# Spreading softmax merge factors: twelve transposes of repeated columns, or one transpose, a store to DRAM and broadcast loads

## The chip, the cores and the metric

The kernel runs on one core of a Trainium2 chip. The metric is device time in microseconds (us) of one execution. Engines are named as in the profile: PE (TensorE matmuls; PEld its weight loads), DVE (VectorE), ACT (ScalarE), POOL (GpSimd) and SP (SyncE, which here only issues DMAs). Each takes its own queue of instructions in order and waits on semaphores where an instruction needs the result of another engine. SBUF is the memory on the chip with 128 partitions, PSUM the eight banks into which PE writes, DRAM the memory outside.

## The reference

Two decoder layers over 1024 tokens of width 1024, in float32. Layer 0 is a gating mixer followed by a squared-ReLU MLP; layer 1 is an attention mixer followed by the same kind of MLP. The change lies in the attention mixer. It has 8 heads of width 64 and three groups of keys (window 128 with stride 1, 512 with stride 4, 2048 with stride 16). For every token and head, each group g gives an unnormalised sum of values, a denominator and a row maximum, and the groups are merged:

```
m_all = jnp.max(jnp.stack(maxs), axis=0)
scales = [jnp.exp(m_ - m_all) for m_ in maxs]
num_sum = sum(n_ * c[..., None] for n_, c in zip(nums, scales))
den_sum = sum(d_ * c for d_, c in zip(dens, scales))
o = (num_sum / den_sum[..., None])
```

So a token's 64 values of a head and group are all multiplied by one number, the factor f = scale / den_sum.

## The kernel before

Heads are taken in pairs hp = 0 to 3, so that a pair's 2 x 64 = 128 channels fill the partitions. A pair and a group is a unit (`U`, with `u.hp`, `u.g`); there are 12 units, and within a pair they come in the order g = 1, 2, 0. For each unit PE forms queries, keys and values from the weights `in_w_qkv` (tiles `mm`, weight halves `wp`, by a scheme of seven products per pair of tiles); these are 128x512 matmuls that keep PE filled. Beside them runs the attention of the units, in steps of 256 tokens: `scores` (PE, tiles `at<-k,q`), the row maxima and exponentials (DVE line 1265, ACT line 1267, tile `st`), `turned` (PE transposes of the probabilities, then a split into a high and a low part, tiles `tr`), and `values` (PE, `at<-tr,V`, then ACT and DVE into the unit's `N`, lines 1304 and 1305). `N` holds channels on partitions and tokens along the row. The factors come from DVE the other way: `f` holds tokens on partitions.

`merge(hp, i)` does the merge of a pair for the token half i (512 tokens, four blocks of 128). It first forms `f` (lines 1402 to 1416), three groups x four blocks x two heads = 24 numbers for each of 128 partitions. To turn them, `factors(g)` lets ACT write each number 64 times side by side (line 1422, 128x512), and `spread_factors` lets PE transpose four 128x128 blocks of that into a PSUM bank, which then holds for each channel (partition) and token the factor. DVE multiplies by it (lines 1439 and 1450), sums the three groups (1443, 1451), and SP stores the result to DRAM (1456) for pairs 0 to 2; pair 3 is split for the output projection. The 8 merges thus hold 8 x 3 x 4 = 96 transposes.

Two things set the order. PE's is written out by hand: a planner (`Flow`) keeps a clock of PE's work, and a generator such as `merge` says with `yield` how many nanoseconds (the table `LAT`) to let pass before its next PE instruction. The attention of the next pair takes its `N` buffer once `merged[hp, 1]` has come. The other engines' order is made by a scheduler when the program is built. Temporary tiles `t` rotate through 11 buffers, `at` through 5 PSUM banks, raw weights `r` through 4 buffers: SP's weight loads (line 169) wait in its queue until DVE has split an earlier one.

## Time and profile before

| | |
|---|---|
| median of 3 runs | 2153.97 us (2151.77 to 2154.95) |
| the profiled execution | 2152.68 us, span 2151.0 us |
| mean granted TensorE clock | 0.992 |
| attention stage | about 956 to 1500 us of the span |
| transposes of tiles `t` (line 187) | 472, from 956 to 1477 us |
| ACT's broadcast copies of `f` (line 1422) | 24, from 1062 to 1472 us |

Busy times are from one profiled execution. A row of a timeline or a group has start or count, length, engine, line, operation, output<-input and shape; what stands in square brackets is idle time of the engine just before, and who ended it. Matmuls overlap, so the recorded length of one is more than what it adds. A wait for several semaphores is put down to the one that came last. For a DMA the time to landing runs from its issue to its completion.

### The profile page before, as it was taken

Reading aid. Unit: us, or ns where it says so; the run is one execution under the profiler, and the core shown is the slowest. Engines: PE = TensorE matmul, PEld = TensorE weight load, DVE = VectorE, ACT = ScalarE, POOL = GpSimd, SP = SyncE. Lnnn points to the kernel's source line nnn. Section 1 sums busy time; section 2 is a strip of 40 time slices with the busy share of each in tenths; the row PEclk is TensorE's granted clock in tenths of the full one; section 3 lists DMA queues with packets and bytes.
Section 4 is the critical chain, followed back from the end, with each engine's and each line's share of the span. In section 5 each row is a group of like instructions: output and inputs, shape, how many; then the busy total and the mean of one; then the engine's idle time right before and its main releaser. Section 6 shows DMA issues by size and latency. Waiting matters only on the chain.

```text
span 2151.0 us, 30121 instructions
## 1 busy us (share of the span) xinstructions
PE 2114.8 (98%) x10242; PEld 1752.0 (81%) x10242; DVE 1636.2 (76%) x3010; ACT 1121.3 (52%) x2261; POOL 562.8 (26%) x417
## 2 busy tenths in 40 slices
PE   8999999999999999999999999999999999999998
PEld 7888887888878888887888788887888888788887
DVE  7975268567699888897787877877866766988886
ACT  7644136555564444346665666664455556544443
POOL 2100113233223333521212122201133332332345
PEclk9999999999999999999999999999999999999999
DMA  6411113455364444221112111150055543644432
GB/s 223 141 59 50 40 47 134 165 189 184 114 195 153 156 157 137 89 93 37 46 46 56 40 47 47 44 182 27 32 176 195 191 158 123 200 153 141 144 106 78
DMA packets 158813, 247.04 MB, mean 115 GB/s; under 512 B 33481, under 2 KB 47940, under 8 KB 158660
## 3 DMA queue, kind: packets, MB, share of 16 engines
q1 hardware_dynamic: 158336, 244.94, 35.1%
q8 instruction: 80, 1.31, 0.3%
q14 instruction: 73, 0.60, 0.1%
q10 hardware_dynamic: 324, 0.18, 0.0%
HBM read 180.41 MB, written 64.66 MB: 114 GB/s over the span
## 4 chain that ended last, share of the span: by engine, by line
PE 87%; DVE 7%; ACT 2%; DMA 2%; issue 2%; SPq 1%; DVEq 0%; ACTq 0%
PE at L180 43%; PE mm L180 41%; PE at L187 2%; DVE wp L206 1%; DMA t<-hid 1%; DVE hx L206 1%; ACT t L1267 1%; DMA r<-in_w_up 1%; DVE h L935 1%; DVE k L1170 0%; DVE q L1170 0%; ACT wp L205 0%; SPq L169 0%; DVE tr L206 0%; DVE h L338 0%
## 5 line engine op out<-in xcount | busy, mean ns | idle before, releaser
L205 ACT ACTIVATE wp<-r 128x512 fp32r<-128x512 f32 (+3 forms) x490 | 294.2, 605 | 450.8 <-PE at L180 289.1
L180 PE MATMUL at<-hx,wp 128*128 128x512 f32 x1770 | 413.8, 389 | 4.6 <-DVE wp L206 2.6
L206 DVE TENSOR_TENSOR wp<-r,wp 128x512 fp32r<-128x512 f32 (+3 forms) x490 | 376.2, 771 | 38.6 <-ACT wp L205 34.9
L180 PE MATMUL mm<-y,wp 128*128 128x512 f32 x1608 | 399.3, 394 | 2.2 <-ACT t L1127 1.0
L180 PEld LDWEIGHTS at<-hx,wp 128*128 128x128 f32 x1770 | 331.8, 188 | 75.8 <-DVE h L935 3.7
L180 PEld LDWEIGHTS mm<-y,wp 128*128 128x128 f32 x1608 | 300.1, 189 | 68.1 <-DVE h L338 1.6
L180 PE MATMUL at<-t,wp 128*128 128x512 f32 x1344 | 314.0, 389 | 0.0
L180 PEld LDWEIGHTS at<-t,wp 128*128 128x128 f32 x1344 | 252.2, 188 | 52.7 <-DVE t L798 0.4
L408 POOL TENSOR_TENSOR t<-r 128x512 f32<-128x512 f32 (+3 forms) x78 | 112.8, 1446 | 677.8 <-DMA r<-in_w_dn 299.2
L410 POOL TENSOR_TENSOR r<-r 128x512 f32<-128x512 f32 (+3 forms) x77 | 115.0, 1493 | 388.7 <-DVE wp L206 352.7
L180 PE MATMUL mm<-t,wp 128*128 128x512 f32 x768 | 192.9, 399 | 0.0
L206 DVE TENSOR_TENSOR hx<-t,hx 128x512 fp32r<-128x512 f32 x192 | 178.5, 942 | 5.9 <-ACT hx L205 5.9
L180 PE MATMUL mm<-hx,wp 128*128 128x512 f32 x708 | 171.7, 389 | 0.1
L180 PEld LDWEIGHTS mm<-t,wp 128*128 128x128 f32 x768 | 141.4, 189 | 30.1 <-issue 0.2
L267 POOL TENSOR_TENSOR t<-t 128x512 f32<-128x512 f32 (+1 forms) x54 | 71.5, 1325 | 354.6 <-ACT t L258 352.9
L180 PE MATMUL mm<-y,whi 128*128 128x512 f32 x512 | 158.3, 390 | 0.0
L180 PEld LDWEIGHTS mm<-hx,wp 128*128 128x128 f32 x708 | 132.7, 188 | 28.1 <-DVE b L961 0.7
L935 DVE TENSOR_TENSOR h<-h,at 128x512 f32<-128x512 f32 x144 | 97.6, 680 | 55.3 <-PE at L180 55.3
L798 DVE TENSOR_TENSOR t<-t,at 128x512 f32<-128x512 f32 x116 | 79.2, 684 | 77.5 <-PE at L180 77.3
L180 PE MATMUL at<-y,wp 128*128 128x512 f32 x552 | 138.1, 391 | 0.0
L205 ACT ACTIVATE hx<-t 128x512 fp32r<-128x512 f32 x192 | 118.3, 629 | 30.6 <-DMA t<-hid 24.1
L413 POOL TENSOR_TENSOR r<-r 128x512 f32<-128x512 f32 (+3 forms) x77 | 105.4, 1369 | 82.7 <-issue 48.2
(221 smaller groups left out, 3198.8 us busy)
## 6 DMA issues: line engine op xcount, KB each, us to landing
t<-hid SPq DMA_DIRECT2D x194, 256.0 KB, 5.1
hid<-t SPq DMA_DIRECT2D x140, 256.0 KB, 2.5
r<-in_w_up SPq DMA_DIRECT2D x128, 256.0 KB, 2.8
r<-in_w_dn SPq DMA_DIRECT2D x88, 256.0 KB, 2.7
r<-in_w_qkv SPq DMA_DIRECT2D x72, 256.0 KB, 2.6
hid<-b SPq DMA_DIRECT2D x56, 256.0 KB, 2.7
r<-in_w_v SPq DMA_DIRECT2D x48, 256.0 KB, 3.9
h<-in_xT SPq DMA_DIRECT2D x16, 256.0 KB, 3.3
```

Source lines behind the costliest of these rows:

```text
L180: nc.tensor.matmul(out, lhsT, rhs, **kw)
L187: nc.tensor.transpose(out, src, ident)
L205: nc.scalar.activation(hi, src, AF.Copy)
L206: nc.vector.tensor_tensor(lo, src, hi.bitcast(F32), op=ALU.subtract)
L267: nc.gpsimd.tensor_tensor(self.acc, self.acc, sq, op=ALU.add)
L408: tt(r7, r[0, 0], r[1, 0], op=ALU.subtract)
L410: tt(r6, r[1, 0], r[0, 0], op=ALU.subtract)
L413: tt(r3, r[0, 1], r6, op=ALU.subtract)
L798: nc.vector.tensor_tensor(out, x, y, op=ALU.add)
L935: engine.tensor_tensor(hs[i, s], hs[i, s], src, op=ALU.add)
L1267: nc.scalar.activation(p[:, c], p[:, c], AF.Exp, bias=m, scale=-1.0, accum_out=dn)
```

## The change

For pairs 0 to 2, `merge` keeps the 24 numbers as one row of 24 columns (`fs`), and PE transposes all of them at once: out come 24 rows of 128 tokens. ACT copies them to SBUF (`ft`), SP stores them to a small DRAM tile (`rows`, 6 rows of 512 tokens: a group and a head each), and SP loads each row back to 64 partitions, two loads for a tile `t` of 128 partitions. DVE multiplies with these tiles in SBUF in place of a PSUM bank. The waits of the planner between the steps are written anew, the last two operations of DVE no longer have a raised priority, and pair 3 stays as it was. Per merge 12 transposes and three 128x512 copies of ACT go; one transpose, one 24x128 copy, one store of 12 KB and six loads of 128 KB come.

```diff
--- before.py
+++ after.py
@@ -1401,10 +1401,11 @@
         mn = small.tile([P, 4, 2], F32, tag="mn", name="mn", bufs=2)
         nc.vector.tensor_tensor(mn, e[0][:, :, :, 0], e[1][:, :, :, 0], op=ALU.min)
         nc.vector.tensor_tensor(mn, mn, e[2][:, :, :, 0], op=ALU.min)
-        f = small.tile([P, 3, 4, 2], F32, tag="f", name="f", bufs=2)
+        fs = small.tile([P, 3, 8], F32, tag="f", name="f", bufs=2)
+        f = fs.rearrange("p g (a b) -> p g b a", a=2) if hp < 3 else fs.rearrange("p g (b a) -> p g b a", a=2)
         for g in range(3):
             nc.vector.tensor_tensor(f[:, g], mn, e[g][:, :, :, 0], op=ALU.subtract)
-        nc.scalar.activation(f, f, AF.Exp)
+        nc.scalar.activation(fs, fs, AF.Exp)
         dn = small.tile([P, 4, 2], F32, tag="dn", name="dn", bufs=2)
         d2 = small.tile([P, 4, 2], F32, tag="d2", name="d2", bufs=2)
         nc.vector.tensor_tensor(dn, f[:, 0], e[0][:, :, :, 1], op=ALU.mult)
@@ -1415,6 +1416,41 @@
         for g in range(3):
             nc.vector.tensor_tensor(f[:, g], f[:, g], dn, op=ALU.mult)
         quick.__exit__(None, None, None)
+        if hp < 3:
+            yield LAT["merge"] + 1500
+            pt = at_bank()
+            transpose(pt[0:24, 0:P], fs.rearrange("p g n -> p (g n)"))
+            ft = small.tile([24, P], F32, tag="ft", name="ft", bufs=1)
+            rows = dram.tile([6, HALF], F32, tag=f"rows{i}", name=f"rows{i}", bufs=1)
+            with tc.high_priority(offset=PRIO):
+                nc.scalar.activation(ft, pt[0:24, 0:P], AF.Copy)
+            nc.sync.dma_start(rows.rearrange("n (b t) -> (n b) t", b=4), ft)
+            yield 5000
+
+            def row(g):
+                x = temp()
+                for a in range(2):
+                    nc.sync.dma_start(x[64 * a:64 * a + 64, :], rows[2 * g + a:2 * g + a + 1, :].partition_broadcast(64))
+                return x
+
+            pbs = [row(1), row(2)]
+            yield 4000
+            for g, pb in zip((1, 2), pbs):
+                nc.vector.tensor_tensor(own(pb, g), permuted(us_[g].N, i, g), own(pb, g), op=ALU.mult)
+            rest = pbs[0]
+            nc.vector.tensor_tensor(rest, rest, pbs[1], op=ALU.add)
+            pb = row(0)
+            yield 3000
+            yield valued[hp, i], 500
+            N = us_[0].N[:, half(i)]
+            nc.vector.tensor_tensor(N, N, pb, op=ALU.mult)
+            nc.vector.tensor_tensor(N, N, rest, op=ALU.add)
+            yield LAT["sum"]
+            if i == 0:
+                kept_N[hp] = dram.tile([P, S], F32, tag=f"N{hp}", name=f"N{hp}", bufs=1)
+            nc.sync.dma_start(kept_N[hp][:, half(i)], N)
+            merged[hp, i].t = flow.t
+            return
         yield LAT["merge"]
         def factors(g):
             fe = temp()
@@ -1430,7 +1466,7 @@
             return pb
 
         rest = None
-        fe_ns = LAT["fe"] * (1.0 if hp == 3 else LAT["fex"])
+        fe_ns = LAT["fe"]
         for g in (1, 2):
             fe = factors(g)
             yield fe_ns
@@ -1450,12 +1486,7 @@
             nc.vector.tensor_tensor(N, N, pb, op=ALU.mult)
             nc.vector.tensor_tensor(N, N, rest, op=ALU.add)
         yield LAT["sum"]
-        if hp < 3:
-            if i == 0:
-                kept_N[hp] = dram.tile([P, S], F32, tag=f"N{hp}", name=f"N{hp}", bufs=1)
-            nc.sync.dma_start(kept_N[hp][:, half(i)], N)
-        else:
-            split_N(hp, i, N)
+        split_N(hp, i, N)
         merged[hp, i].t = flow.t
 
     outs = {}
```

The planner lays PE's work out anew around the merges. In the order of PE, at the first merge (pair 0, half 0; `t_8784` and the like are inputs of the query, key and value products, `tr` probabilities), before:

```order
L180 MATMUL mm<-t_8784,wp 128x512 x3
L180 MATMUL mm<-t_8787,wp 128x512 x3
L180 MATMUL mm<-t_8658,wp 128x512 x3
L187 MATMUL at<-ident,t 128x128 x4
L180 MATMUL mm<-t_8674,wp 128x512 x3
L180 MATMUL mm<-t_8690,wp 128x512 x3
L180 MATMUL mm<-t_8702,wp 128x512 x3
L187 MATMUL at<-ident,t 128x128 x4
L180 MATMUL at<-tr,V 128x256 x2
```

and with the change:

```order
L180 MATMUL mm<-t_8784,wp 128x512 x3
L180 MATMUL mm<-t_8787,wp 128x512 x3
L187 MATMUL at<-ident,f 24x128
L180 MATMUL mm<-t_8658,wp 128x512 x3
L187 MATMUL at<-ident,t 128x128 x4
L180 MATMUL mm<-t_8674,wp 128x512 x3
L180 MATMUL mm<-t_8690,wp 128x512 x3
L180 MATMUL mm<-t_8702,wp 128x512 x3
L180 MATMUL mm<-y,wp 128x512 x3
```

The one transpose of `f` stands 12 matmuls of 512 columns and a group of transposes (that of V) ahead of where the first group of factors stood, and that group is gone. In the order of DVE, a little later in the same merge, before:

```order
L1439 TENSOR_TENSOR t<-N,at 128x512
L1443 TENSOR_TENSOR t<-t 128x512
L1202 TENSOR_TENSOR t<-t,mm 128x512
L206 TENSOR_TENSOR wp<-r,wp 128x512
L206 TENSOR_TENSOR tr<-at,tr 128x512 x2
```

and with the change:

```order
L1202 TENSOR_TENSOR t<-t,mm 128x512
L206 TENSOR_TENSOR wp<-r,wp 128x512
L1439 TENSOR_TENSOR t<-N,t 128x512
L206 TENSOR_TENSOR wp<-r,wp 128x512
L1439 TENSOR_TENSOR t<-N,t 128x512
L1441 TENSOR_TENSOR t<-t 128x512
L206 TENSOR_TENSOR tr<-at,tr 128x512 x2
```

Both multiplies (line 1439) now stand between a reduction of scores and the split of the probabilities `tr`; before, the first of them stood ahead of the reduction. In the order of SP, for the two merges of pair 0, with the change (`bvec` is the bias table, `N_10047` the result):

```order
L169 DMA r<-in_w_qkv 128x512
L1427 DMA rows_9770<-ft 24x128
L1433 DMA t<-rows_9770 64x512 x4
L169 DMA r<-in_w_qkv 128x512 x2
L1433 DMA t<-rows_9770 64x512 x2
L169 DMA r<-in_w_qkv 128x512
L1451 DMA N_10047<-N 128x512
L169 DMA r<-in_w_qkv 128x512
L1427 DMA rows_10123<-ft 24x128
L1433 DMA t<-rows_10123 64x512
L1066 DMA t<-bvec 64x2x64 x2
L1433 DMA t<-rows_10123 64x512 x5
```

Before, only the weight loads, the bias loads and the stores of `N` stood there; the stores and loads of `rows` are new, and share the queue with the weight loads.

## The prediction

> **What bounds the kernel now.** First the page: engines and the chain of waits.
>
> ```profile
> span 2151.0 us, 30121 instructions
> PE 2114.8 (98%) x10242; PEld 1752.0 (81%) x10242; DVE 1636.2 (76%) x3010; ACT 1121.3 (52%) x2261; POOL 562.8 (26%) x417
> ...
> PE 87%; DVE 7%; ACT 2%; DMA 2%; issue 2%; SPq 1%; DVEq 0%; ACTq 0%
> ```
>
> PE is busy for 98% of the span and holds 87% of the chain that ended last. The change touches one stage, so next the table by stretches, for the attention stage (columns: stretch, length, busy time of PE, PEld, DVE, ACT, POOL, then PE clock, DMA share, GB/s), and what PE waited for there (total us, times, longest).
>
> ```profile
> 956.00:1500.00 544.00, 529.27 (x3079) 440.80 (x3078) 438.94 (x1097) 337.95 (x868) 93.81 (x65) 0.98 0.20 58
> ```
> ```profile
> PE at L180 <- DVE tr L206: 3.5, 4, 1.1
> PE at L180 <- DVE q L1170: 2.4, 3, 1.0
> PE at L187 <- ACT t L1422: 2.1, 1, 2.1
> ```
>
> In this stage PE idles 544 - 529.27 = 14.7 us, in pieces of at most 2.1 us, and DVE is busy 439 of 544 us (81%), ACT 62%, the DMA engines 20%. So PE bounds the stage, with DVE not far behind it, and an instruction taken off PE shortens the span unless another engine then makes PE wait. The profiled execution took 2152.68 us, 1.3 us (0.06%) under the median 2153.97 of the runs; sums below start from 2152.68. What a measurement of this kernel can tell from no change is about 0.2%, 4.3 us.
>
> **PE: the term of the gain.** Each of the six merges of head pairs 0 to 2 loses three groups of four transposes and gains one transpose. The record of a transpose is not its price, since matmuls overlap; the price is the shift of what follows. In PE's timeline (start, length, engine, line, operation, shape, count):
>
> ```profile
> 1061.08 3.70 PE L180 MATMUL mm<-t,wp 128*128 128x512 f32 x15
> 1064.62 0.60 PE L187 MATMUL at<-ident,t 128*128 128x128 f32 x4
> 1064.97 2.31 PE L180 MATMUL mm<-t,wp 128*128 128x512 f32 x9
> 1067.12 0.60 PE L187 MATMUL at<-ident,t 128*128 128x128 f32 x4
> 1067.48 1.12 PE L180 MATMUL at<-tr,V 128*128 128x256 f32 x8
> ...
> 1148.04 3.57 PE L180 MATMUL mm<-t,wp 128*128 128x512 f32 x15
> 1151.44 1.03 PE L187 MATMUL at<-ident,t 128*128 128x128 f32 x8
> 1152.23 2.31 PE L180 MATMUL mm<-t,wp 128*128 128x512 f32 x9
> ```
> ```profile
> 143.01 134.07 PE mm L180 x591
> ```
>
> The chain's row gives 134.07 / 591 = 0.227 us from one 512-column matmul to the next. From 1061.08 to 1064.97 are 3.89 us, of which 15 x 0.227 = 3.40 belong to matmuls: four transposes cost 0.49. From 1064.97 to 1067.48, 2.51 - 9 x 0.227 gives 0.47. Eight cost 1152.23 - 1148.04 - 3.40 = 0.79. So a group costs about 0.17 plus 0.08 for each transpose. Removed: 6 x 3 x 0.48 = 8.6 us. Added: one transpose, 0.08 where it stands beside others, 0.25 alone; nearly alone is nearer, 6 x 0.24 = 1.4. Net **-7.2 us**, with ends -7.0 and -8.2.
>
> The records themselves are longer:
>
> ```profile
> L187 PE MATMUL at<-ident,t x472: 270/273/477, 956.4 to 1477.0; 128*128 128x128 f32 x158
> ```
>
> At 0.273 us each, 66 fewer would be 18.0 us; the shifts above, 0.08 to 0.12 us a transpose, say that most of a record overlaps the next, so I keep 7.2 and leave the other to the rivals. The Trainium skill prices a transpose by the record: its page "TensorE: Matmul & The Clock Gate", Part 4 (PE-mode transpose), has about 275 ns inside a kernel, most of it access latency, which would make it an estimated 18.2 us; this trace agrees on the length, and not on the price.
>
> **ACT and DVE.** Now their groups (duration min/median/max in ns) and the DMAs nearest to the new ones.
>
> ```profile
> L1422 ACT ACTIVATE t<-f x24: 613/618/643, 1062.0 to 1472.0; 128x512 f32<-128x512 f32 x24
> L1407 ACT ACTIVATE f<-f x8: 206/219/225, 1057.6 to 1460.3; 128x24 f32<-128x24 f32 x8
> L1439 DVE TENSOR_TENSOR t<-N,at x16: 958/1074/1093, 1068.6 to 1475.0; 128x512 f32<-128x512 f32 x16
> L1443 DVE TENSOR_TENSOR t<-t x8: 682/692/1777, 1073.8 to 1476.1; 128x512 f32<-128x512 f32 x8
> L1450 DVE TENSOR_TENSOR N<-N,at x8: 671/678/683, 1082.3 to 1477.5; 128x512 f32<-128x512 f32 x8
> L1389 SPq DMA_DIRECT2D ex<-sc x8: 377/382/391, 1007.2 to 1430.2; - x8
> L1387 SPq DMA_DIRECT2D sc<-st x8: 551/590/633, 1037.8 to 1426.3; - x8
> DMA to landing us min/median/max: 2.2/2.6/3.3
> ```
>
> ACT loses 18 broadcast copies of 0.618 us (11.1 us) and gains six small copies between 0.22 (L1407's row) and 0.62: 1.3 to 3.7 us. ACT idles 38% of the stage, so this counts as nothing; at most it shortens some of PE's 14.7 us of waits. DVE keeps its five large operations of a merge. Their second operand moves from PSUM to SBUF: L1443 reads SBUF alone at 692 ns, L1450 reads PSUM at 678, so 18 multiplies change by between +0.25 us and nothing. The strided f rows of 24 elements stay near 0.16 us. All this lies beside PE, at 0.
>
> **SP.** It gains 6 stores and 36 loads of 128 KB. By the rows of the small DMAs an issue takes 0.38 to 0.59 us, 42 of them 16 to 25 us of SP's time. In the stage, SP mostly waits for buffers of weights:
>
> ```profile
> SPq L169 <- DVE wp L206: 286.6, 54, 33.9
> ```
>
> The loads bring 36 x 128 KB = 4.7 MB, over the stage 9 GB/s beside the table's 58 at a DMA share of 0.20: hidden.
>
> **The new wait.** The factors used to reach DVE through PE and PSUM; now they go ACT, store, load. What is queued behind DVE's multiply (L1439) are the splits of probabilities (tr) for PE's next product with the values, then the score sums. So is the load in time? For the first merge:
>
> ```profile
> 1060.41 0.32 DVE L1416 TENSOR_TENSOR f<-f,dn 128x8 f32<-128x8 f32 x3
> 1075.45 0.69 DVE L206 TENSOR_TENSOR wp<-r,wp 128x512 fp32r<-128x512 f32 x1 [0.32 <-ACT wp L205]
> 1077.89 1.29 DVE L206 TENSOR_TENSOR tr<-at,tr 128x512 fp32r<-128x512 f32 x2 [1.75 <-ACT tr L205]
> ```
> ```profile
> 1064.13 0.63 ACT L205 ACTIVATE wp<-r 128x512 fp32r<-128x512 f32 x1 [1.52 <-PE mm L180]
> ```
> ```profile
> 1062.56 0.33 SPq L169 DMA_DIRECT2D r<-in_w_qkv  x1
> ```
>
> f is ready at 1060.7. In the new order PE transposes it 12 matmuls after 1061.08, at 1063.8; ACT has the split of 1064.13 ahead of the copy, so the copy ends by 1065.1. SP's last issue ahead is that of 1062.56, so the store goes out at once and lands 2.2 to 3.3 us later, at 1067.3 to 1068.4. Four load issues (1.5 to 2.4) and a landing (2.2 to 3.3) bring both tiles by 1071.0 to 1074.1. The new DVE order puts the first multiply behind the split of 1075.45, at 1076: 1.9 us of margin at the worst. The third factor's loads stand behind two weight loads, but have until about 1082 (the first start of L1450). In merge (0,1) two bias loads stand between the halves of a tile (see the order of SP above):
>
> ```profile
> 1100.57 1.28 SPq L1066 DMA_DIRECT2D t<-bvec  x2
> ```
> ```profile
> 1107.91 1.01 DVE L206 TENSOR_TENSOR tr<-at,tr 128x384 fp32r<-128x384 f32 x2
> ```
>
> They are issued by 1101.9, three more issues of rows end at 1103.0 to 1103.6, and the tiles land at 1105.2 to 1106.9. The multiply stands behind the tr pair that ends at 1108.9, earlier by at most the two or so microseconds that PE has gained by then: little margin, but some. So I price late rows at 0 to 2 us per merge and take none.
>
> What does move is where the multiplies stand: both now come right ahead of the tr pair, 1.07 us plus a weight split of 0.69, 1.76 more than before, and the idle time there is 1.75 (the row of 1077.89). That place already cost PE something:
>
> ```profile
> 1078.64 0.97 PE L180 MATMUL at<-k,q 64*128 64x256 f32 x11 [0.67 <-DVE tr L206]
> ```
>
> So the cover is used up and no more. Ends: 0, and 1.76 at each of six merges, 10.6 us. The first is nearer, since the slack equals the push; I take 0.25 per merge, **+1.5 us**. Below nothing: freed PSUM banks (three per merge to one) and ACT time could remove waits, at most the 14.7 us.
>
> The planner's longer waits (5000, 4000, 3000 ns) hold no engine by themselves: they only decide what PE finds next in its queue.
>
> **Sum.** 2152.68 - 7.2 + 1.5 = 2147.0 us, that is -5.7 us on the profiled execution, and 0.32% under the median.
>
> **The rivals.**
>
> *The gain turns into waits.* PE comes to tr, q and the score products earlier, but DVE and ACT do not; DVE at 81% in the stage and PE's 3.5 + 2.4 us of waits for tr and q speak for it, the 19% idle of DVE against. If 1.0 us per merge is given back, 2152.68 - 7.2 + 6.0 = 2151.5: no change that can be told. Chance 0.25.
>
> *Late rows stop DVE.* SP issues in order; a store that has to wait for ACT, or loads behind a weight load that waits for a buffer (33.9 us at the longest), hold the rows, the multiply waits at the head of DVE's queue, and PE runs out of tr. It pays from 7.2 / 6 = 1.2 us per merge on, and slower can be told from 1.9. If one load's landing, 2.6 us, is exposed per merge, 2152.68 - 7.2 + 15.6 = 2161.1. Against it: the margins worked out above. Chance 0.15.
>
> The Trainium skill sides with this rival: "DMA: Bandwidth & Descriptors", Anatomy of one DMA, gives every DMA a fixed cost of about 2 us, mostly the receipt of the write, and here two follow each other. The rows above agree, at 2.2 to 3.3 us. By the page's figure the pair takes some 4 us, which fits the margins.
>
> *Waits go too.* The freed banks and ACT take away a third of the stage's 14.7 us: 2152.68 - 7.2 - 4.9 = 2140.6. That the waits name DVE's tr and q, not banks, speaks against it. Chance 0.05.
>
> *A transpose costs its record.* 2152.68 - 18.0 + 1.5 = 2136.2. The shifts speak against it. Chance 0.03.
>
> **How the numbers follow.** Forecast 0.52 (own range 2143.5 to 2149.5), gain into waits 0.25, late rows 0.15, waits go too 0.05, a transpose at its record 0.03. Faster by over 0.2% (under 2149.7): 0.52 + 0.05 + 0.03 = 0.60. Within 0.2%: 0.25. Slower: 0.15. The range from 2142 to 2159 takes in the second case and the milder part of the third, and leaves out the worst of late rows and the last two cases.
>
> **What would show it.** Right: L187 with 66 fewer matmuls, PE's busy time in the stage down by about what its length is, no wait of DVE on a load of rows above 1 us, PE's idle time still near 15 us. Wrong in the sum: matmul starts around the removed groups closer by other than 0.48 us. Wrong by the rivals: DVE L1439 waiting for a DMA by several us per merge, or PE's waits for tr, q and k up by 6 us or more, with the stage as long as before. If the stage is shorter and the span isn't, the tail behind the last unit has taken it back.

## The result, and the profile after

The changed kernel takes 2161.93 us (median of 7 runs, 2158.17 to 2163.88), the kernel before in the same session 2152.33 (7 runs, 2147.93 to 2154.95): a ratio of 1.0040, 95% interval 1.0030 to 1.0051. It is slower by 9 us where 6 to 7 us of gain were forecast. The profiled execution of it took 2161.58 us.

First the same three views as before: the head and the chain of the page, the attention stage in the table by stretches, and what PE waited for in the stage (us in total, times, longest).

```profile
span 2159.9 us, 30068 instructions
PE 2114.0 (98%) x10176; PEld 1747.9 (81%) x10176; DVE 1640.2 (76%) x3010; ACT 1113.3 (52%) x2249; POOL 566.3 (26%) x417
...
PE 82%; DVE 10%; ACT 4%; issue 2%; DMA 1%; POOL 0%; SPq 0%; DVEq 0%; ACTq 0%; POOLq 0%
```
```profile
956.00:1500.00 544.00, 520.04 (x2966) 429.44 (x2965) 435.67 (x1088) 325.85 (x849) 91.30 (x63) 0.97 0.23 67
```
```profile
PE at L180 <- DVE tr L206: 8.9, 6, 2.1
PE at L187 <- ACT t L1267: 3.9, 9, 1.5
PE at L180 <- DVE k L1170: 2.4, 3, 0.9
PE at L187 <- ACT t L1458: 2.1, 1, 2.1
```

and one more row of the kernel before:

```profile
PE at L187 <- ACT t L1267: 0.5, 3, 0.2
```

PE has 66 instructions fewer (10242 to 10176) and hardly less busy time, and its share of the chain fell from 87% to 82%, most of which went to DVE and ACT. The wait for `tr` grew from 3.5 to 8.9 us, and a wait for the exponentials (line 1267), 0.5 us before, is 3.9.

A stretch with fixed ends does not hold the same work in two kernels. So here is PE from 956 us to the same matmul behind the stage, the one that waits 0.74 us for `h` of line 338: first the kernel before, then the changed one (stretch, length, PE busy, granted clock, DMA share, GB/s).

```profile
956.00:1491.19 535.19, 520.46 (x3028) 0.98 0.21 59
```
```profile
956.00:1499.56 543.56, 519.60 (x2965) 0.97 0.23 67
```

The stage is 8.4 us longer: 0.9 us less busy time and 9.2 us more idle time (535.19 - 520.46 = 14.7, and 543.56 - 519.60 = 24.0). Behind the stage the two agree within 0.6 us. Why does busy time fall by 0.9 and not by 7? Mostly because the clock is lower. Added up over stretches of 5 us, each at 1 minus its granted clock, the stage of the kernel before loses 10.2 us to the clock and the changed one 15.4. Without that, busy time falls by 6.1. In the traces the loss comes in pieces of 3.41 us, or whole multiples of it, at half of the clock, 1.7 us each: six of them in the stage before, nine after.

Not all of this belongs to the change. Up to the matmul that starts at 1062.32 us in the kernel before and at 1063.38 us in the changed one, PE's instructions are the same, in the same order, and already there the two executions differ. From one matmul near 956 us to that one it takes 106.1 and 106.7 us, with 3.9 and 5.7 us of idle time and 5.1 and 3.4 us lost to the clock. Where the clock was lower PE waited less, so idle time and lost clock should be read together. From there, "from the first merge on" below, to the same matmul behind the stage, before and after:

```profile
1062.32:1491.19 428.87, 418.07 (x2468) 0.99 0.21 62
```
```profile
1063.38:1499.56 436.18, 417.91 (x2403) 0.97 0.25 72
```

This part is 7.3 us longer: idle time is 18.3 us in place of 10.8 (7.5 more), the clock takes 11.9 in place of 5.1 (6.8 more), and busy time without that falls by 7.0. By the same working the stretch ahead, which holds the same work, reads 0.5 us apart in these two executions and up to 1.5 in all kernels of this document, so the 7.0 is good to about a microsecond.

One of the new stalls, in DVE's timeline of the changed kernel and then in PE's (start, length, engine, line, operation, shape, count, idle time before and who ended it), and the clock there:

```profile
1108.75 0.29 DVE L1071 COPY b<-t 128x256 f32<-128x256 f32 x1 [1.95 <-DMA t<-bvec]
1108.96 1.01 DVE L206 TENSOR_TENSOR tr<-at,tr 128x384 fp32r<-128x384 f32 x2
1109.89 1.09 DVE L1439 TENSOR_TENSOR t<-N,t 128x512 f32<-128x512 f32 x1
1111.25 1.08 DVE L1439 TENSOR_TENSOR t<-N,t 128x512 f32<-128x512 f32 x1 [0.27 <-DMA t<-rows]
1112.25 0.28 DVE L1265 CUSTOM_DVE_ANT_0 t<-at,b 128x128 f32<-128x128 f32 x1
...
1120.91 0.53 DVE L206 TENSOR_TENSOR tr<-at,tr 128x384 fp32r<-128x384 f32 x1
```
```profile
1121.50 1.14 PE L180 MATMUL at<-tr,V 128*128 128x256 f32 x8 [2.00 <-DVE tr L206]
1123.34 2.06 PE L187 MATMUL at<-ident,t 128*128 128x128 f32 x6 [0.70 <-ACT t L1267]
...
1126.90 4.34 PE L180 MATMUL mm<-y,wp 128*128 128x512 f32 x12
```
```profile
1120.00:1125.00 5.00, 2.79 (x14) 0.79 0.14 52
1125.00:1130.00 5.00, 5.00 (x22) 0.52 0.01 3
```

DVE waits 1.95 us for a bias load, then does the `tr` pair and both multiplies of line 1439, and only at 1112.25 comes to the row maxima (line 1265) of the next scores. From there it works nearly without a gap, the other three operations of this merge among it, until `tr` at 1120.91, and PE stands 2.00 us. (ACT, which makes the high part of `tr`, waited 2.64 us for DVE's line 1166 in between.) Then the clock falls: twelve 512-column matmuls take 4.34 us, which elsewhere take 3.04. The 10 us from 1120 to 1130 lose 2.2 us to idle time and 0.21 x 5 + 0.48 x 5 = 3.45 us to the clock.

What the change added is small (ns min/median/max of one; the landing times are those of the loads of line 1433; then DVE's wait for rows in the stage):

```profile
L187 PE MATMUL at<-ident,f x6: 271/272/387, 1065.0 to 1357.9; 128*24 128x128 f32 x6
L1433 SPq DMA_DIRECT2D t<-rows x36: 444/588/620, 1070.1 to 1370.0; - x36
DMA to landing us min/median/max: 2.8/3.2/4.1
```
```profile
DVE t L1439 <- DMA t<-rows: 0.5, 2, 0.3
```

DVE waited only 0.5 us in all for rows. The new path was in time; the time was lost elsewhere. What did grow is DVE's wait for bias loads (line 1071), first before, then after:

```profile
DVE b L1071 <- DMA t<-bvec: 2.6, 2, 1.4
```
```profile
DVE b L1071 <- DMA t<-bvec: 8.2, 5, 2.1
```

### The profile page after: what moved, and what is told of

Its sections match the earlier page's. It is cut to its first block, busy times and chain, and to the rows that moved or that the text cites. A ratio compares the mean times of both kernels' runs of the same rounds, so it can differ in the third digit from the quotient of the medians.

```text
span 2159.9 us, 30068 instructions
## 1 busy us (share of the span) xinstructions
PE 2114.0 (98%) x10176; PEld 1747.9 (81%) x10176; DVE 1640.2 (76%) x3010; ACT 1113.3 (52%) x2249; POOL 566.3 (26%) x417
## 4 chain that ended last, share of the span: by engine, by line
PE 82%; DVE 10%; ACT 4%; issue 2%; DMA 1%; POOL 0%; SPq 0%; DVEq 0%; ACTq 0%; POOLq 0%
PE at L180 41%; PE mm L180 39%; DVE wp L206 2%; PE at L187 2%; ACT wp L205 1%; DVE hx L206 1%; ACT t L1267 1%; DVE h L935 1%; DVE k L1170 1%; DMA r<-in_w_up 1%; DVE t L206 1%; DVE h L338 0%; DVE tr L206 0%; DVE q L1170 0%; ACT q L1169 0%
```

## The experiments

All ratios are to the kernel before in the same session. The count of matmuls in another place is taken from the order of PE's 9730 matmuls of line 180 in the traces, position by position against the kernel before, with buffer numbers left out; transposes are not counted. The changed kernel has 300 in another place.

### The waits on the old path, and three causes on the new one

**The waits of the change on the old path.** The kernel before with its twelve transposes, and the changed kernel's waits between them. It takes over more than the waits: the first two groups are multiplied one right after the other, and the last two operations of DVE have no raised priority, both as in the changed kernel.

```diff
+        if hp < 3:
+            yield 1500
+            fes = [factors(1), factors(2)]
+            yield 9000
...
+            fe = factors(0)
+            yield 3000
+            yield valued[hp, i], 500
```

> The kernel before, with its 12 transposes and PSUM banks, but with the planner's waits of the changed kernel around them (and both factor groups multiplied one after the other). Theory DVE (the merge's operations stand late and together in DVE's queue, ahead of the splits of probabilities and the score reductions, because their operands come by DMA; PE then waits and its clock halves): the operands come from PE again, so at most +3 us on the kernel before. Theory SP (the 42 added DMAs hold SP's queue, and bias tiles and weights come late): no added DMA, so 0. Theory planner (the new waits alone make the order of PE worse): +8 us or more.

Measured: 2160.55 us, ratio 1.0031 (1.0019 to 1.0042), with 192 matmuls in another place. PE's aligned stage:

```profile
956.00:1499.51 543.51, 523.35 (x3034) 0.98 0.21 58
```

Idle time is 20.2 us against 14.7, and busy time, with the same number of matmuls and transposes, 2.9 us more. No factor travels through DRAM here, and a loss of 0.31% is there.

**No trip through DRAM.**

DVE multiplies by a tile of ones, so this kernel leaves the factors out of the result of pairs 0 to 2.

```diff
-            nc.sync.dma_start(rows.rearrange("n (b t) -> (n b) t", b=4), ft)
...
-                x = temp()
-                for a in range(2):
-                    nc.sync.dma_start(x[64 * a:64 * a + 64, :], ...)
-                return x
+                n = (128, 32)[g - 1]
+                return ones[:, 0:n, None].to_broadcast([P, n, DIL[g]])
...
+                x = temp()
+                nc.vector.tensor_tensor(own(x, g), permuted(us_[g].N, i, g), pb, op=ALU.mult)
...
+            nc.vector.tensor_tensor(N4, N4, ones[:, None, :].to_broadcast([P, 4, P]), op=ALU.mult)
```

> The changed kernel without the store and the six loads of each merge: DVE multiplies by a tile of ones instead of the factors (so the factors are left out of the result of pairs 0 to 2). The transposes saved and the planner's waits stay. Theory SP: -6 us on the kernel before. Theory DVE: -4 to -7 us, since the multiplies wait for nothing and the scheduler can place them in gaps. Theory planner: +6 us or more.

Measured: 2161.69 us, ratio 1.0042 (1.0027 to 1.0056). PE's order is that of the changed kernel, row for row. The loss stays whole, so neither the added DMAs on SP nor DVE's wait for rows makes it.

**The multiplies off DVE.**

```diff
-                nc.vector.tensor_tensor(own(pb, g), permuted(us_[g].N, i, g), own(pb, g), op=ALU.mult)
+                nc.gpsimd.tensor_tensor(own(pb, g), permuted(us_[g].N, i, g), own(pb, g), op=ALU.mult)
...
-            nc.vector.tensor_tensor(rest, rest, pbs[1], op=ALU.add)
+            nc.gpsimd.tensor_tensor(rest, rest, pbs[1], op=ALU.add)
```

> The changed kernel with the two multiplies by factors 1 and 2 and their sum on POOL in place of DVE; the DMAs are the same. Theory DVE: 17 us of DVE's work leave the places before tr and the score sums, so -3 to -7 us on the kernel before. Theory SP: +7 to +10 us as the changed kernel. Theory planner: +7 us or more.

Measured: 2158.77 us, ratio 1.0020 (1.0010 to 1.0030). PE's order is that of the changed kernel, row for row. About half of the loss goes with three operations of DVE, so DVE's queue is part of it.

**Other DMA queues.** The store on ACT's queue, the loads on POOL's.

```diff
-            nc.sync.dma_start(rows.rearrange("n (b t) -> (n b) t", b=4), ft)
+            nc.scalar.dma_start(rows.rearrange("n (b t) -> (n b) t", b=4), ft)
...
-                    nc.sync.dma_start(x[64 * a:64 * a + 64, :], ...)
+                    nc.gpsimd.dma_start(x[64 * a:64 * a + 64, :], ...)
```

> The changed kernel with the store of the rows issued by ACT and their loads by POOL, so SP's queue is what it was before. Theory SP: DVE's waits for bias tiles go back from 8.2 to about 2.6 us and the time to -4 us or lower against the kernel before. Theory DVE: the multiplies still stand where they stood, so +5 to +10 us. Theory planner: +7 us or more.

Measured: 2161.96 us, ratio 1.0038 (1.0024 to 1.0053). SP's queue is not the cause. The sign that the expectation set, DVE's waits for bias loads back at 2.6 us, did not come: they are 7.2 us here. In the first kernel of this section, which adds no DMA at all, they are 9.9 us. So the added DMAs are not needed for the late bias loads; these come with the planner's waits too.

### Is PE's removed work worth anything, and do the old waits repair it?

**Giving PE its work back.** Twelve transposes of the identity in each merge, whose result nobody reads.

```diff
+            for _ in range(3):
+                dm = at_bank()
+                for b in range(4):
+                    transpose(dm[:, blk(b)], ident)
```

> The changed kernel with its waits, plus twelve transposes of the identity per token half, into three buffers that nobody reads, placed where the two factor rows are multiplied: TensorE gets the removed work back, nobody waits for its results. Theory 'paid by TensorE' (each removed transpose was worth its 0.12 us, so that giving 72 of them back costs 8.6 us): 2170 against the changed kernel's 2162, +0.7% on the kernel before. Theory 'TensorE stands anyway' (with the late waits the removed work only left longer standstills): the twelve fill standstills, 2160 to 2163, no more than +0.1% on the changed kernel.

Measured: 2168.9 us, ratio 1.0076 (1.0062 to 1.0089). That is 0.36%, or 7.7 us, on the changed kernel. PE's order moves with it too (223 matmuls in another place, 300 in the changed kernel), so this is not the price of the transposes alone, but it is near the 8.6 us of the prediction, and more than nothing, which it would be if the twelve only filled standstills.

**The waits of before on the new path.**

```diff
-            yield LAT["merge"] + 1500
+            yield LAT["merge"]
...
-            yield 5000
...
-            yield 4000
+            yield 6000
...
+                if g == 1:
+                    yield 1800
...
-            yield 3000
-            yield valued[hp, i], 500
+            yield 3900
+            yield valued[hp, i], 0
...
+            with tc.high_priority(offset=PRIO):
...
```

The last two operations of DVE have their raised priority again, here and in all kernels below that are made from this one.

> The changed kernel with the planner's waits of the kernel before: the transpose comes after the plain wait for the merge, the store and four loads go out in one piece, the two multiplies come 6000 and 7800 ns after, N's multiply 3900 ns after that and with priority, the last wait as before; in all the total of before. Theory 'the planner's waits' (the longer waits cost about 8 us and the transposes' work is a gain of 6 to 7 as predicted): the loss is gone and the gain stands, 2146 to 2150, ratio to before 0.9965 to 0.999. Theory 'the new path itself' (DMA hop, rows and its spots on VectorE cost whatever the waits): 2158 to 2163, ratio 1.002 or more. If the waits are only half of it: 2153 to 2156.

Measured: 2160.81 us, ratio 1.0034 (1.0023 to 1.0045). The expectation missed something simple, which PE's waits show:

```profile
PE at L187 <- DVE f L1417: 12.4, 3, 10.0
PE at L180 <- DVE tr L206: 2.4, 3, 1.0
```

The wait for `tr` is back to 2.4 us, but the transpose now stood where ACT's broadcast copy used to stand, 3900 ns of the planner ahead of the old transposes, and PE waited 12.4 us for the factors themselves.

**The same, multiplies and sum on GpSimd** (the edit as above).

> As the kernel with the waits of before, and the two multiplies by the rows and their sum run on GpSimd in place of VectorE; TensorE's order is the same. Theory 'VectorE's queue' (the multiplies of 1.08 and the sum of 0.68 us stand ahead of what TensorE waits for): 3 us less than the kernel with those waits on VectorE, the size seen when the changed kernel's multiplies moved (2161.9 to 2158.8). Theory 'planner's waits alone': within 1 us of it.

Measured: 2159.9 us, ratio 1.0032 (1.0017 to 1.0046). No difference that can be told; DVE is not what holds this one.

**The kernel before, two factor groups together.**

```diff
+        both = {}
+        if hp < 3:
+            both = {g: factors(g) for g in (1, 2)}
+            yield 2 * fe_ns
         for g in (1, 2):
-            fe = factors(g)
-            yield fe_ns
+            fe = both[g] if hp < 3 else factors(g)
+            if hp == 3:
+                yield fe_ns
```

> The kernel before with all its transposes and its total waits; only the first two factor groups are spread and multiplied together where the second stood, in place of one after the other. Theory 'bunched' (two multiplies and a sum of 2.9 us in one piece on VectorE hold TensorE): +4 us or more of the 6.6 that the waits cost on the kernel before, ratio 1.002 to 1.003. Theory 'late' (the later end of the merge moves the matmuls that fill TensorE): ratio 0.9995 to 1.0005.

Measured: 2158.99 us, ratio 1.0028 (1.0017 to 1.0038), with 168 matmuls in another place. By the expectation this spoke for the bunch of 2.9 us on DVE. The next runs took that back.

### Bunched, late, or just another order?

**The transpose where the changed kernel has it, the end where the kernel before has it**: as the kernel with the waits of before, with `yield LAT["merge"] + 1500` ahead of the transpose and 4500 in place of 6000.

> The changed kernel with the single transpose where the changed kernel has it (so that TensorE does not wait for the factors, 12.4 us in the kernel with the waits of before), the store and loads at once, the multiplies 4500 and 6300 ns after, N's multiply 3900 after that with priority: the end of the merge where it was in the kernel before, and the two multiplies 1.8 us apart. Theory 'late and bunched' (the waits cost it, by the late end or by 2.9 us of VectorE in one piece): 2146 to 2152, ratio below 1.000. Theory 'any other order loses what the order of before had' : 2157 to 2162, ratio 1.002 to 1.004.

Measured: 2152.22 us, ratio 0.9997 (0.9988 to 1.0006). The loss is gone and no gain is there: PE is idle for 537.05 - 517.41 = 19.6 us.

```profile
956.00:1493.05 537.05, 517.41 (x2964) 0.97 0.23 68
```

**The same with the multiplies on GpSimd.**

> As the kernel with the total of before, with the two multiplies and the sum on GpSimd; TensorE's order stays. Theory 'VectorE's queue': 3 us less than with the multiplies on VectorE, so 2144 to 2149 if that one is at 2147 to 2152, 2155 to 2159 if it is at 2158 to 2162. Theory 'order': the same as it within 1 us.

Measured: 2155.05 us, ratio 1.0006 (0.9997 to 1.0014). PE's order is the same; taking the three operations from DVE helps nothing here.

**The kernel before, ending later.**

```diff
-        yield LAT["sum"]
+        yield LAT["sum"] + (1900 if hp < 3 else 0)
```

> The kernel before with all its parts, and only the last wait of a merge 1900 ns longer, as much as the changed kernel's merge ends later; TensorE's order changes in two places by one group of three matmuls. Theory 'late end': ratio 1.001 to 1.003. Theories 'bunched' and 'order': 0.9995 to 1.0007.

Measured: 2154.01 us, ratio 0.9999 (0.9990 to 1.0008). On the old path a late end alone costs nothing.

**The kernel before, all three waits longer.**

```diff
-        fe_ns = LAT["fe"] * (1.0 if hp == 3 else LAT["fex"])
+        fe_ns = LAT["fe"] * (1.0 if hp == 3 else LAT["fex"] + 0.4)
```

> The kernel before with all its parts; each of the three waits for the factors is 4420 ns in place of 3900, so that the multiplies stay apart but come later, and the merge ends 1560 later: another order (TensorE's rows differ in some 200 lines, the bunched kernel's in some 390) without a bunch. Theory 'bunched': 0.9993 to 1.0007. Theories 'late end' and 'any other order loses': 1.0015 to 1.003.

Measured: 2154.97 us, ratio 1.0008 (0.9999 to 1.0017), with 102 matmuls in another place.

**The changed kernel, only its multiplies apart.**

```diff
-            yield 5000
+            yield 3200
...
+                if g == 1:
+                    yield 1800
```

> The changed kernel with one edit: its two multiplies 1800 ns apart in the planner instead of in one piece; the wait ahead of the loads is 1800 shorter, so that the second multiply, the late end and N's place stay. Theory 'bunch': most of the loss is gone, 2152 to 2156, ratio 1.000 to 1.0015. Theory 'late end and N's place': 2159 to 2163, ratio 1.003 to 1.004.

Measured: 2165.13 us, ratio 1.0054 (1.0042 to 1.0066): slower than the changed kernel, by about 3 us. PE's waits for `tr` are 9.7 us. With this "bunched" falls as the cause of the changed kernel's loss; what the bunch cost on the old path is not told apart from the other order there.

**The old path at the waits that gave 0.9997.**

```diff
-            yield fe_ns
+            yield fe_ns if hp == 3 else (6000, 1800)[g - 1]
```

> The kernel before with all twelve transposes, its factor groups spread and multiplied 6000 and 7800 ns after the merge's wait, so that multiplies, N's multiply and the end stand where the new path has them at ratio 0.9997 (there the transpose is earlier). Theory 'path is worth 7 us, the order costs it': 2158 to 2162, ratio 1.002 to 1.004. Theory 'the path gives nothing, whatever the order': 2151 to 2155, within 0.05% of the new path with these waits.

Measured: 2161.37 us, ratio 1.0037 (1.0025 to 1.0049). PE's stage and its longest waits:

```profile
956.00:1498.28 542.28, 520.40 (x3031) 0.98 0.20 58
```
```profile
PE at L187 <- ACT t L1267: 7.1, 10, 1.6
PE at L180 <- DVE tr L206: 3.6, 4, 1.2
```

Busy time is that of the kernel before to 0.1 us, with all its transposes, and idle time is 21.9 us in place of 14.7: 7.2 us more, of which 5.3 lie behind the first merge's start. This is the cleanest test of the waits, since nothing else is edited here, neither the path nor a priority nor a bunch. PE waits for the exponentials, not for `tr`; so each kernel has its own place where it loses. And its 9730 matmuls of line 180 stand in the very order of the kernel with all three waits longer, which read 1.0008; only transposes stand elsewhere among them. So this order alone does not decide. At the same waits the new path is 0.40% faster, but the two orders of PE are not the same (210 of the 9730 matmuls stand elsewhere), so that is no clean price either.

**Multiplies 3900 ns apart on the new path**: as the kernel at 0.9997, with 3900 in place of 1800 between the multiplies; and once more with 1800 in place of 3900 ahead of N's multiply, which puts the end back.

> The new path with the multiplies 4500 and 8400 ns after the loads are issued, 3900 apart as in the kernel before, and all after them 2100 later. Theory 'the closer to before's spacing the more of the 7 us stays': 2146 to 2150, ratio 0.997 to 0.999. Theory 'the gain is taken by waits anyway': 2151 to 2155, ratio 0.999 to 1.001.

Measured: 2158.84 us, ratio 1.0025 (1.0015 to 1.0035).

> As the kernel with multiplies 3900 apart, with N's multiply 1800 instead of 3900 ns after the second, so that the merge ends as in the kernel before. By the first theory 2145 to 2150, by the second 2151 to 2155; a later end of 2100 alone, which cost the kernel before nothing, should make no difference of more than 1 us between this and that one.

Measured: 2154.74 us, ratio 1.0003 (0.9994 to 1.0013). Neither has a gain, so the spacing decides nothing. A later end of 2100 ns goes with 0.2% here, against the expectation; 1900 ns were harmless to the kernel before.

### The order held

In these two the planner does not see that anything was removed. The single transpose stands where the first group of four stood, the planner's clock is moved on by the eleven that are gone, and all waits are as before.

```diff
-            yield LAT["merge"] + 1500
+            yield LAT["merge"]
+            wait = LAT["fe"] * LAT["fex"]
+            yield wait
...
             transpose(pt[0:24, 0:P], fs.rearrange("p g n -> p (g n)"))
+            flow.pe(3 * TRANSPOSE)
...
-            yield 5000
...
             pbs = [row(1), row(2)]
-            yield 4000
+            yield wait
+            flow.pe(4 * TRANSPOSE)
...
-            yield 3000
-            yield valued[hp, i], 500
+            yield wait
+            yield valued[hp, i], 0
             N = us_[0].N[:, half(i)]
...
+            flow.pe(4 * TRANSPOSE)
+            with tc.high_priority(offset=PRIO):
...
```

In the traces all 9730 matmuls of line 180 (the expectation says 9653) then stand in exactly the order of the kernel before.

> The new path with the planner blind to it: the single transpose where the first factor group's transposes stood, the planner's clock moved on by the eleven transposes that are gone, and the waits of before, so that all 9653 matmuls of TensorE stand in exactly the order of the kernel before; store and loads at once, both multiplies where the second stood, N's multiply with priority. Theory 'order' (the removed work is worth 7 to 8.6 us, and the changed kernel's other order of the matmuls takes it and more): 2145 to 2149, ratio 0.996 to 0.998, idle time of TensorE up to 1500 us as before at 15 to 17 us. Theory 'new path' (the trip through DRAM and VectorE's longer piece make TensorE wait whatever the order): 2153 to 2160, ratio 1.000 or more, idle time 20 us or more.

Measured: 2151.12 us, ratio 0.9984 (0.9974 to 0.9994), faster than both kernels. Its stage and PE's longest waits there:

```profile
956.00:1485.05 529.05, 510.35 (x2964) 0.99 0.23 69
```
```profile
PE at L180 <- DVE tr L206: 5.1, 4, 1.5
PE at L187 <- ACT t L1463: 2.1, 1, 2.1
PE at L187 <- ACT t L1267: 2.0, 4, 1.5
PE at L180 <- DVE q L1170: 1.9, 3, 0.7
```

Busy time is 510.35 against 520.46, or 10.1 us less. Of that 3.4 us are the clock (6.8 against 10.2 us lost), and 6.7 us are the removed work. Idle time is 529.05 - 510.35 = 18.7 us, 4.0 more than before, between the two theories' figures; the ratio too lies between their ranges, 0.996 to 0.998 and 1.000 or more. From the start of the first merge on the parts are these:

```profile
1063.25:1485.05 421.80, 408.84 (x2402) 0.99 0.25 75
```

Idle time is 13.0 us there, 2.2 more than before, the clock takes 3.4 in place of 5.1, and the removed work is 7.5. This execution, at 2145.68 us, was the fastest of its 12; the medians give a gain of 3.4 us.

**The same, the second multiply 1800 ns later.**

> The same, with the second multiply 1800 ns after the first in the planner's time; all matmuls again in the order of the kernel before. Theory 'order': within 2 us of it, 0.996 to 0.998. If VectorE's bunch matters where the order is held: 2 us or more below it. Theory 'new path': 1.000 or more.

Measured: 2156.5 us, ratio 1.0009 (1.0000 to 1.0018).

```profile
956.00:1492.94 536.94, 515.27 (x2966) 0.98 0.23 68
```

Idle time is 21.7 us, with all of PE's instructions in the same order. So PE's order is not the whole of it either: in the traces 40 of DVE's 3010 operations stand in another place than in the kernel just above, and 3.0 us more of PE's idle time went with it. By the expectation this ratio is the figure of "new path". Here the rows were late. DVE waited 3.0 us for them in the kernel just above, and 5.3 us in this one:

```profile
DVE t L1442 <- DMA t<-rows: 3.2, 7, 0.8
DVE N L1453 <- DMA t<-rows: 2.1, 1, 2.1
```

The loads of the third factor are issued behind the second multiply, so that this edit also brings them 1800 ns nearer to N's multiply. How much of the loss is the late rows, and how much the other places, is not shown.

## Why the prediction was wrong, step by step

| kernel | path | matmuls in another place | ratio | PE idle in the stage, us | of it from the first merge on, us | lost to the clock in the span, us |
|---|---|---|---|---|---|---|
| before | old | 0 | 1 | 14.7 | 10.8 | 14.5 to 16.4 |
| late end | old | 30 | 0.9999 | 14.9 | 10.8 | 17.0 |
| longer waits | old | 102 | 1.0008 | 15.7 | 11.7 | 16.6 |
| waits of the 0.9997 kernel | old | 102 | 1.0037 | 21.9 | 16.1 | 17.3 |
| two groups together | old | 168 | 1.0028 | 19.4 | 13.7 | 17.4 |
| waits of the change | old | 192 | 1.0031 | 20.2 | 14.5 | 17.5 |
| order held | new | 0 | 0.9984 | 18.7 | 13.0 | 18.6 |
| order held, apart | new | 0 | 1.0009 | 21.7 | 15.9 | 18.8 |
| end as before | new | 272 | 0.9997 | 19.6 | 13.8 | 19.8 |
| multiplies 3900 apart, end as before | new | 272 | 1.0003 | 19.9 | 16.0 | 19.0 |
| the change | new | 300 | 1.0040 | 24.0 | 18.3 | 23.8 |
| multiplies 3900 apart | new | 312 | 1.0025 | 19.3 | 15.3 | 22.9 |
| the change, apart | new | 318 | 1.0054 | 22.4 | 18.5 | 28.6 |

Idle times are from one execution each, at the aligned stage, and can differ from the medians by some microseconds; up to the first merge they are 3.6 to 4.1 us in some executions and 5.6 to 5.9 in others, of the same instructions of PE. The last column is the mean over all executions of a kernel of 1 minus the granted clock, times the span (for the kernel before, over those of five sessions); the clock is on record to three decimals, which is 1 us either way in one execution.

The last column has something that one execution cannot show. All experiments on the new path lose more to the clock than the kernel before in their own session, by 2.6 to 12.7 us, the held order 3.0; on the old path it is 0.8 to 2.9. The changed kernel, in whose session no clock of the kernel before is on record, is 7.4 to 9.3 us above the five others. Taken off the mean span, the lost clock leaves 2135.9 to 2137.0 us for the kernel before, 2136.4 for the changed one, 2130.3 for the held order (2136.6 before in its session), and 2142.8 for the one-line edit of the waits on the old path (2136.2). By this working, waits used up the removed work in the changed kernel, and its net loss is about as large as the clock's; with the order held 6.3 us of the work show, and the clock takes 3.0 back; the one-line edit loses 6.6 us to waits and 1.4 to the clock. The working takes the whole lost clock as lost time, which is the most that it can be. Why the new path has the lower clock is not shown.

*PE bounds the stage*: right. Twelve idle transposes per merge made the kernel 7.7 us slower, and the held order brought a gain.

*The removed work, -7.2 us*: right. From the first merge on and without the clock's part it measured -7.5 with the order held, -6.6 in that kernel's variant and -7.0 in the changed kernel (-6.7 and -6.1 over the whole stage for the first and the last). By the records of 0.273 us it would have been 18 us; that rival falls. (By the prediction's own prices its lower end is 7.1, not 7.0.)

*ACT and DVE at 0*: nearly. Line 1439 went from 1074 to 1082 ns. ACT's busy time in the whole span fell by 8.0 us, and no gain from it shows.

*SP, and rows in time*: right for the changed kernel, with less to spare on the way. The first load went out at 1070.1 us, where the store was to land by 1068.4 at the latest, and the loads took 2.8 to 4.1 us to land, where 2.2 to 3.3 were set. (The section of the Trainium skill that the prediction cites for about 2 us, "DMA: Bandwidth & Descriptors", Anatomy of one DMA, describes DMAs on GpSimd's path; these are issued by SP.) DVE still waited only 0.5 us for rows, no trip through DRAM left the loss whole, and so did other queues. In the kernels with the order held DVE waited 3.0 and 5.3 us for rows; there they were late. The rival of late rows gave 2161.1, within a microsecond of the measured time, and for the wrong reason.

*Two multiplies ahead of `tr`, +1.5 us*: not settled as a number. On GpSimd they took half of the loss with them in the changed kernel, nothing in two others, and apart they were worse.

*"The planner's longer waits (5000, 4000, 3000 ns) hold no engine by themselves: they only decide what PE finds next in its queue."* **This is the step that failed.** It was priced at nothing. What PE finds next is what its idle time is made of. On the old path a one-line edit of the waits cost 0.37%, and the changed kernel's waits, with its bunch and without the raised priority, 0.31%. The new path with the old waits and the old order of matmuls came out at 0.9984, with the changed kernel's at 1.0040, a difference of 0.56%, some 12 us. On PE's side, from the first merge on, idle time rose by 7.5 us and the lower clock added 6.8, where the sum had 1.5 for the one and no term for the other; with 7.0 of work removed, that is 7.3 us. (Over the whole stage it is 9.2, 5.2 and 6.1, and 8.4 us.)

So the rival "the gain turns into waits" had the right kind of loss and less than half of the size: it set 1 us per merge, and it was 7.5 / 6 = 1.2 of idle time plus 1.1 of clock. Its sign came: PE's waits for `tr`, `q` and `k` rose from 3.5 + 2.4 + 0.7 = 6.6 to 8.9 + 1.4 + 2.4 = 12.7 us, by the 6 us that the prediction had set. But it looked at engines that would not keep up with a faster PE. With the order held that is 2.2 to 5.1 us of idle time; the rest in the changed kernel came with the queues in another order and the same engines late at other places.

What stays open is which trait of an order costs. The late end, the bunch, and the spacing were each tried and none decides. Nor is it the order of PE's matmuls alone: the same order read 1.0008 and 1.0037 on the old path, and with the order held 0.9984 and 1.0009. On the new path it goes with the time more closely, though not wholly: kernels of one order read 0.9997, 1.0003 and 1.0006 with the end as before, 1.0032 and 1.0034 with the waits of before, and 1.0020 to 1.0042 with the order of the changed kernel, whichever queues or engines did its loads and multiplies. The raised priority of the last two operations, which the change dropped and the better kernels have again, was not tried by itself. It did not save the kernels at 1.0025 and 1.0034, which have it. That the order of the kernel before stands at the good end of those seen here is shown by the table, where all other orders of the old path but the nearly unchanged one read higher, the kernel at 1.0008 within its interval. Why it does is not shown.

## What to carry to other kernels

When a change alters the numbers from which a planner or a scheduler sets the order, price the other order by itself: here other waits, with the little that was edited beside them, moved the time by up to 0.4% on the old path and 0.7% on the new one, more than the 0.3% that the removed work was worth. To measure what a removed piece of work is worth, hold the order, for example by letting the planner go on booking the time of what is gone; only then was a gain seen here. Compare the granted clock of all executions before reading one trace: here the execution that was profiled with the order held had lost less to the clock than the kernel before, and the mean of its 12 had lost more. And when several experiments that change the order by one trait all read slower, suspect that the starting order was good before believing in the trait: here the bunched multiplies looked like the cause until they were taken apart.

## What the runs showed of the hardware

The clock of PE halves behind stalls far shorter than 3 us, and not behind each of them. The same matmul of the first merge is stalled nearly alike in the changed kernel and in the order-held one; the rows of PE, and the table by stretches around them (busy time, granted clock, DMA share, GB/s), for the changed kernel:

```profile
1080.77 0.98 PE L180 MATMUL at<-k,q 64*128 64x256 f32 x11 [1.27 <-DVE tr L206]
1081.68 4.59 PE L180 MATMUL mm<-t,wp 128*128 128x512 f32 x12
```
```profile
1080.00:1085.00 5.00, 4.23 (x19) 0.70 0.24 81
1085.00:1090.00 5.00, 5.00 (x31) 0.96 0.20 52
```

and for the kernel with the order held:

```profile
1079.62 0.98 PE L180 MATMUL at<-k,q 64*128 64x256 f32 x11 [1.28 <-DVE tr L206]
1080.52 4.38 PE L180 MATMUL mm<-t,wp 128*128 128x512 f32 x18
```
```profile
1078.00:1083.00 5.00, 3.72 (x24) 1.00 0.19 52
1083.00:1088.00 5.00, 5.00 (x34) 1.00 0.28 90
```

In the one, twelve matmuls take 4.59 us and 0.30 x 5 + 0.04 x 5 = 1.7 us are lost to the clock; in the other, eighteen take 4.38 us at full clock. So a stall of 1.3 us may cost 1.7 us on top of itself; what decides it is not shown. Nor is all that the clock takes lost time: the same instructions ahead of the first merge took 106.1 us with 5.1 us lost to the clock and 3.9 of idle time, and 106.7 with 3.4 and 5.7. The Trainium skill, "TensorE: Matmul & The Clock Gate", Why this matters for your kernels, says to avoid gaps of more than about 3 us; here shorter ones cost too.
